# Moving the first loads of a two-layer hybrid block between two DMA-issuing engines

## The chip, the cores and the metric

The kernel runs on one core of a Trainium2 chip. A core has TensorE (PE in the profile, with its weight loads shown apart as PEld), VectorE (DVE), ScalarE (ACT), GpSimd (POOL) and the Sync engine (SP). Transfers are issued by SP or by ScalarE and carried by 16 DMA engines. The metric is the device time of one execution in microseconds. An execution under the profiler gives a trace as well; its times in the text are counted from the start of the profiled span.

## The reference

Two layers work on 512 tokens of width 1024, all in float32. Each layer normalises its input, projects it, mixes tokens (layer A by a chunked spatial gate, layer B by attention with forgetting), attends to 256 memory rows, projects back, and runs a gated feed-forward network. Only the very first step matters here:

```python
h = x
a = rmsnorm(h, ln_mix_pre[0])
mem_n = rmsnorm(mem, ln_mem[0])
proj = a @ w_in_a[0]
u, v, q_mem = proj[..., :768], proj[..., 768:1536], proj[..., 1536:]
...
h = h + rmsnorm(mixed @ w_out[0], ln_mix_post[0])
```

`rmsnorm` scales each token by the inverse root of its mean square and each feature by a gain.

## The kernel before

Activations lie transposed: the features are on the 128 partitions, in eight tiles (`k` = 0 to 7) of 128 features by 512 tokens. `h` holds all eight; it begins as the input `x`. In float32 the products are made from parts. Every operand is split into a high part, rounded to `fp32r`, and the low remainder, and each product is three matmuls: high by high, high by low, low by high. ScalarE writes the high part and VectorE then computes the low one, by `split` for weights (lines 238 and 239: `whi`, `wlo` from `raw`) and by `scaled_parts` for activations (lines 243 and 244: `ahi`, `alo` from `h`, with a gain from the tile `gains` as the scale). The token's own factor of the norm is applied after the products, so these do not wait for the sums of squares.

The work begins with a warm-up: line 82 queues 20 matmuls on a tile of zeros, 256 columns wide (`idle`), on TensorE. ScalarE issues the load of `gains` (all the norms' gains, 48 KB) and then loads its function table ahead of a first tiny activation (`early`). The rest is in `layer_a`. Its first stage computes the two query tiles of the memory attention: two outputs, eight tiles of features each, three products for each pair, so 48 products of 512 columns. Some of the first half are issued as two halves of 256 columns (`HALVES`). The loop goes over halves of the features (`k` 0 to 3, then 4 to 7), inside it over the two outputs, then over `k`, then over the three products; inputs are used in that order.

`query_weights(m, c0, c1)` loads columns of the weights of output `m` and splits them; 128 columns belong to one `k`. `tokens(k0, k1)` loads tiles of `x` and makes their parts. Both queue their loads on SP, in the order of the program. Thus SP's order is: weights 0 for `k` 0 to 3, `x` tiles 0, 1, 2, 3, weights 1 for `k` 0 to 3, weights 0 for `k` 4 to 7, `x` 4 and 5, `x` 6 and 7, weights 1 for `k` 4 to 7, and then the value weights (line 152) and the memory rows (line 345). A tile of `x` is 256 KB, as is one of these pieces of weights.

Behind the first stage come the value products of `value_block` (the tile `v`), and among them the column sums of the squares of `h` (line 288, tile `st`), which need the running sum `acc` that VectorE builds at line 277. `issue_after` and the helper `behind` only set the order in which an engine's instructions are queued; they add no wait for the earlier instruction's end. The framework orders what is left free by a priority that follows the program.

Of the kernel before, what the change touches and what calls it, by code (L numbers as in the profile page):

```python
# [7 lines left out]
F32 = mybir.dt.float32  # L8
F32R = mybir.dt.float32r
BF16 = mybir.dt.bfloat16  # L10
AF = mybir.ActivationFunctionType
# [4 lines left out]
P = 128  # L16
T = 512
D = 1024
KT = 8
# [21 lines left out]
def hybrid(ctx: ExitStack, tc: tile.TileContext, i: dict, out: bass.AP):  # L41
    nc = tc.nc
    cp = ctx.enter_context(tc.tile_pool(name="const", bufs=1))
# [9 lines left out]
    last_load, last_exp, last_parts = [None], [None], [None, None]  # L53

    def name(s):
        n_of[s] = n_of.get(s, 0) + 1
        return f"{s}_{n_of[s]}"

    def act(s, dt=F32R, shape=(P, T)):
        return ap.tile(list(shape), dt, tag="a", name=name(s))  # L60
# [13 lines left out]
    def ps(tag, shape=(P, T), s="ps"):  # L74
        return pp.tile(list(shape), F32, tag=tag, name=name(s), bufs=2 if tag == "tr" else 3)

    V, A, PE, G = nc.vector, nc.scalar, nc.tensor, nc.gpsimd

    def zeros():
        t = plain("zeros", dt=BF16)  # L80
        V.memset(t, 0.0)
        return t

    def idle(n, t, behind=None, width=T):

        def run():
            o = ps("tr", s="idle")
            for _ in range(n):
                PE.matmul(o[:, :width], t[:, :P], t[:, :width], start=True, stop=True)
        if behind is None:  # L90
            return run()
        with tc.issue_after(behind.ins):
            run()

    zero = zeros()
    idle(20, zero, width=T // 2)


    gains = cp.tile([P, 11 * 8 + 8], F32, name="gains")
    nc.scalar.dma_start(gains, i["gains"])  # L100

    def gain(block, k):
        c = block * KT + k
# [17 lines left out]
    avg = cp.tile([P, 1], F32, name="avg")  # L121
# [3 lines left out]
    rms_eps = cp.tile([P, 1], F32, name="rms_eps")  # L125
    V.memset(rms_eps, RMS_EPS)
    early = cp.tile([P, 1], F32, name="early")
    A.activation(early, avg, AF.Copy, scale=2.0)


    def pair_of_parts(n=512, aside=False):
        if aside:
            return act("whi"), act("wlo")
        return (wp.tile([P, max(n, 512)], F32R, tag="hi", name=name("whi"), bufs=8)[:, :n],
                wp.tile([P, max(n, 512)], F32R, tag="lo", name=name("wlo"), bufs=8)[:, :n])

    def cut(pair, w):

        return [(pair[0][:, d : d + w], pair[1][:, d : d + w]) for d in range(0, pair[0].shape[1], w)]
# [98 lines left out]
    def split(src, hi, lo, eng=None):  # L238
        last_parts[:] = A.copy(hi, src), (eng or V).tensor_sub(lo, src, hi)  # L239
# [6 lines left out]
    @contextmanager  # L246
    def behind(some):

        with ExitStack() as s:
            for ins in some:  # L250
                s.enter_context(tc.issue_after(ins.ins))
            yield
# [71 lines left out]
            return [self.sq[0, cols][:, 0, tb * P - cols[0] : (tb + 1) * P - cols[0]]]  # L324


    h = cp.tile([P, KT, T], F32, name="h")
    rbc = cp.tile([P, T], F32, name="rbc")

    def normed_parts(block, k, cols, hi, lo):  # L330
        c0, c1 = cols
        scaled_parts(h[:, k, c0:c1], gain(block, k), hi[:, c0:c1], lo[:, c0:c1])
# [256 lines left out]
    def layer_a():  # L589
# [2 lines left out]
        pre.done = False  # L592
        wq, raws = ([], []), [wp.tile([P, 1024], F32, tag="raw", name=name("raw"), bufs=4) for _ in range(2)]

        def query_weights(m, c0, c1):
            last_load[0] = nc.sync.dma_start(raws[m][:, c0:c1], i["w_a_q"][m][:, c0:c1])
            for c in range(c0, c1, 512):
                pair = pair_of_parts()
                split(raws[m][:, c : c + 512], *pair)
                wq[m].extend(cut(pair, P))  # L600

        def tokens(k0, k1):
            nc.sync.dma_start(h[:, k0:k1, :], i["x"][:, k0:k1, :])
            for k in range(k0, k1):
                normed_parts(G_MIX_PRE, k, FULL, *a[k])

        query_weights(0, 0, 512)
        for k in range(4):
            tokens(k, k + 1)
        query_weights(1, 0, 512)  # L610
        query_weights(0, 512, 1024)
        tokens(4, 6)
        tokens(6, 8)
        last_a = tuple(last_parts)
        query_weights(1, 512, 1024)
# [29 lines left out]
        with tc.tile_pool(name="sgu", bufs=1) as lp:  # L645
# [23 lines left out]
            for half in range(0, KT, 4):  # L669
                for o, w in zip(outs, wq):  # L670
                    for k in range(half, half + 4):
                        for n, (x, y) in enumerate(((0, 0), (0, 1), (1, 0))):
                            first = k == n == 0
                            for c0, c1 in (HALVES if half == 0 and not first else (FULL,)):
                                PE.matmul(o[:, c0:c1], w[k][x], a[k][y][:, c0:c1], start=first,
                                          stop=k == KT - 1 and n == 2, skip_group_check=c1 - c0 < T)
# [110 lines left out]
            for n in range(2):  # L787
# [5 lines left out]
                for g in range(3):  # L793
                    c = bsp[:, 3 * n + g, :]
# [591 lines left out]


    phase = layer_a()

    def memory():  # L1390
# [38 lines left out]
    zero = zeros()  # L1429
# [70 lines left out]
```

## Time and profile before

| | |
|---|---|
| median of 3 runs | 1105.0 us (1104.49 to 1106.13) |
| profiled execution | 1104.96 us |
| its span in the profile | 1103.2 us |
| TensorE busy | 1094.7 us, 99% of the span |
| VectorE, ScalarE busy | 887.8 us, 680.1 us |
| read from HBM | 105.23 MB, 97 GB/s over the span |

A row of the timeline reads: start, time from the first start to the last end of the merged instructions, engine, source line, operation, output and inputs, their number, and in brackets how long the engine had been idle before and what released it. SPq and ACTq are the queues of SP and of ScalarE that issue transfers. A matmul's end is modelled, so its time includes the way through the array: two matmuls that follow each other start closer together than one lasts.

### The profile page before, as it was taken

What the parts mean: (1) busy time and instruction counts of PE and PEld (TensorE: products, weight loads), DVE (VectorE), ACT (ScalarE), POOL (GpSimd) and SP (SyncE); (2) the same over time, 40 slices, a digit from 0 to 9 for tenths busy, and PEclk for the clock granted to TensorE, in tenths of its full rate; (3) what the DMA queues carried; (4) which work ended last, traced back from release to release, by engine and by line L of the source; (5) the groups of instructions that cost most, each with busy time, mean ns of one, the idle gap of its engine ahead of it and who ended that gap; (6) DMA issues with size and microseconds to landing.
All of it is one profiled execution on the core that took longest, in us unless ns stands there. A gap on an engine that the chain in (4) does not pass through costs nothing.

```text
span 1103.2 us, 19498 instructions
## 1 busy us (share of the span) xinstructions
PE 1094.7 (99%) x7363; PEld 1001.1 (91%) x7364; DVE 887.8 (80%) x1750; ACT 680.1 (62%) x1428; POOL 24.4 (2%) x40
## 2 busy tenths in 40 slices
PE   9999999999999999999999999999999999999998
PEld 7998889999899899998988998889999899899996
DVE  7879759997698588797968789868998698588776
ACT  7776578664365254477747788868665266255454
POOL 0000000000000000001000000000000000000000
PEclk9999999999999999999999999999999999999999
DMA  7521331334134133245222654531235134233232
GB/s 269 161 80 54 119 115 39 116 115 136 56 115 144 54 109 115 77 153 175 73 81 61 155 133 121 148 115 40 78 93 157 58 114 132 62 114 116 77 97 77
DMA packets 64021, 118.65 MB, mean 108 GB/s; under 512 B 5236, under 2 KB 40072, under 8 KB 63928
## 3 DMA queue, kind: packets, MB, share of 16 engines
q1 hardware_dynamic: 63032, 116.57, 34.8%
q8 instruction: 58, 0.95, 0.4%
q0 software_dynamic: 192, 0.52, 0.2%
q10 hardware_dynamic: 704, 0.32, 0.1%
q14 instruction: 35, 0.29, 0.1%
HBM read 105.23 MB, written 2.10 MB: 97 GB/s over the span
## 4 chain that ended last, share of the span: by engine, by line
PE 95%; ACT 2%; DVE 2%; DMA 0%; issue 0%; SPq 0%; DVEq 0%; ACTq 0%
PE y L191 10%; PE y L193 10%; PE y L192 10%; PE a L191 5%; PE a L193 5%; PE a L192 5%; PE ps L191 4%; PE ps L193 4%; PE ps L192 4%; PE e L191 3%; PE e L193 3%; PE e L192 3%; PE x L193 3%; PE x L191 3%; PE x L192 3%; PE v L191 2%
## 5 line engine op out<-in xcount | busy, mean ns | idle before, releaser
L239 ACT CAST whi<-raw 128x512 fp32r<-128x512 f32 x460 | 277.9, 621 | 260.7 <-PE y L193 118.5
L239 DVE TENSOR_TENSOR wlo<-raw,whi 128x512 fp32r<-128x512 f32 x460 | 307.4, 690 | 116.6 <-ACT whi L239 114.5
L191 PE MATMUL y<-whi,fhi 128*128 128x512 f32 (+1 forms) x356 | 139.6, 393 | 0.0
L193 PE MATMUL y<-whi,flo 128*128 128x512 f32 (+1 forms) x356 | 139.4, 391 | 0.0
L192 PE MATMUL y<-wlo,fhi 128*128 128x512 f32 (+1 forms) x356 | 139.3, 391 | 0.0
L193 PE MATMUL x<-xshi,wlo 128*128 128x256 f32 x320 | 89.8, 281 | 0.0
L191 PE MATMUL x<-xshi,whi 128*128 128x256 f32 x320 | 89.7, 280 | 0.0
L191 PE MATMUL a<-xshi,whi 128*128 128x256 f32 x320 | 89.7, 281 | 0.0
L192 PE MATMUL a<-xslo,whi 128*128 128x256 f32 x320 | 89.7, 280 | 0.0
L192 PE MATMUL x<-xslo,whi 128*128 128x256 f32 x320 | 89.7, 280 | 0.0
L193 PE MATMUL a<-xshi,wlo 128*128 128x256 f32 x320 | 89.7, 281 | 0.0
L193 PEld LDWEIGHTS y<-whi,flo 128*128 128x128 f32 x356 | 66.9, 188 | 15.6 <-DVE flo L239 0.2
L192 PEld LDWEIGHTS y<-wlo,fhi 128*128 128x128 f32 x356 | 66.9, 188 | 14.8 <-DVE wlo L239 0.2
L191 PEld LDWEIGHTS y<-whi,fhi 128*128 128x128 f32 x356 | 66.9, 188 | 14.7
L191 PE MATMUL ps<-xshi,whi 128*128 128x256 f32 (+1 forms) x224 | 68.4, 305 | 0.0
L192 PE MATMUL ps<-xslo,whi 128*128 128x256 f32 (+1 forms) x224 | 66.6, 298 | 0.0
L193 PE MATMUL ps<-xshi,wlo 128*128 128x256 f32 (+1 forms) x224 | 66.3, 298 | 0.0
L191 PEld LDWEIGHTS a<-xshi,whi 128*128 128x128 f32 x320 | 60.3, 188 | 0.3
L192 PEld LDWEIGHTS a<-xslo,whi 128*128 128x128 f32 x320 | 60.2, 188 | 0.4
L193 PEld LDWEIGHTS x<-xshi,wlo 128*128 128x128 f32 x320 | 60.2, 188 | 0.0
L191 PEld LDWEIGHTS x<-xshi,whi 128*128 128x128 f32 x320 | 60.2, 188 | 0.0
L193 PEld LDWEIGHTS a<-xshi,wlo 128*128 128x128 f32 x320 | 60.2, 188 | 0.0
(303 smaller groups left out, 3080.3 us busy)
## 6 DMA issues: line engine op xcount, KB each, us to landing
raw<-in_w_gate SPq DMA_DIRECT2D x44, 512.0 KB, 3.6
raw<-in_w_up SPq DMA_DIRECT2D x44, 512.0 KB, 3.6
raw<-in_w_down SPq DMA_DIRECT2D x44, 512.0 KB, 4.2
raw<-in_w_out SPq DMA_DIRECT2D x16, 512.0 KB, 3.9
raw<-in_w_b_q SPq DMA_DIRECT2D x8, 512.0 KB, 4.4
raw<-in_w_a_v SPq DMA_DIRECT2D x6, 512.0 KB, 8.2
raw<-in_w_a_u SPq DMA_DIRECT2D x6, 512.0 KB
raw<-in_w_v SPq DMA_DIRECT2D x6, 512.0 KB, 3.5
```

The costliest lines, as they stand in the source:

```text
L191: PE.matmul(o, w[0], x[0], start=start, stop=False, skip_group_check=more)
L192: PE.matmul(o, w[0], x[1], start=False, stop=False, skip_group_check=more)
L193: return PE.matmul(o, w[1], x[0], start=False, stop=stop, skip_group_check=more)
L239: last_parts[:] = A.copy(hi, src), (eng or V).tensor_sub(lo, src, hi)
```

## The change

ScalarE issues `x` tiles 0 and 1 as its first instructions, and tile 3 behind the tiny activation that follows its table load. `gains` moves to SP. The first weights are loaded in two halves of 256 columns (128 KB each), each split by itself; the second half's split is queued behind the parts of tile 1, and the weights of output 1 behind the parts of tile 3. SP's order becomes: weights 0 for `k` 0 and 1, `gains`, weights 0 for `k` 2 and 3, `x` 2, weights 1 for `k` 0 to 3, weights 0 for `k` 4 to 7, and from there on as it was. The warm-up has 16 matmuls in place of 20. In the first stage the three products of a pair are made in the order high by high, low weights by high input, high weights by low input, where the last two stood the other way round.

```diff
-    idle(20, zero, width=T // 2)
+    idle(16, zero, width=T // 2)
...
-    nc.scalar.dma_start(gains, i["gains"])
+    h = cp.tile([P, KT, T], F32, name="h")
+    for k in range(2):
+        nc.scalar.dma_start(h[:, k : k + 1, :], i["x"][:, k : k + 1, :])
...
-    A.activation(early, avg, AF.Copy, scale=2.0)
+    with tc.issue_after(A.activation(early, avg, AF.Copy, scale=2.0).ins):
+        nc.scalar.dma_start(h[:, 3:4, :], i["x"][:, 3:4, :])
...
-        def query_weights(m, c0, c1):
+        def query_weights(m, c0, c1, after=()):
             last_load[0] = nc.sync.dma_start(raws[m][:, c0:c1], i["w_a_q"][m][:, c0:c1])
             for c in range(c0, c1, 512):
-                pair = pair_of_parts()
-                split(raws[m][:, c : c + 512], *pair)
+                n = min(512, c1 - c)
+                pair = pair_of_parts(n)
+                with behind(after):
+                    split(raws[m][:, c : c + n], *pair)
                 wq[m].extend(cut(pair, P))
 
         def tokens(k0, k1):
-            nc.sync.dma_start(h[:, k0:k1, :], i["x"][:, k0:k1, :])
+            if k0 not in (0, 1, 3):
+                nc.sync.dma_start(h[:, k0:k1, :], i["x"][:, k0:k1, :])
             for k in range(k0, k1):
                 normed_parts(G_MIX_PRE, k, FULL, *a[k])
 
-        query_weights(0, 0, 512)
-        for k in range(4):
+        query_weights(0, 0, 256)
+        nc.sync.dma_start(gains, i["gains"])
+        for k in range(2):
             tokens(k, k + 1)
-        query_weights(1, 0, 512)
+        query_weights(0, 256, 512, tuple(last_parts))
+        for k in range(2, 4):
+            tokens(k, k + 1)
+        query_weights(1, 0, 512, tuple(last_parts))
         query_weights(0, 512, 1024)
         tokens(4, 6)
         tokens(6, 8)
...
-                        for n, (x, y) in enumerate(((0, 0), (0, 1), (1, 0))):
+                        for n, (x, y) in enumerate(((0, 0), (1, 0), (0, 1))):
```

More of the change, by code (lines that the diff above doesn't have):

```diff
@@ L324, in sums @@
             return [self.sq[0, cols][:, 0, tb * P - cols[0] : (tb + 1) * P - cols[0]]]
-    h = cp.tile([P, KT, T], F32, name="h")
     rbc = cp.tile([P, T], F32, name="rbc")
```

## The prediction, made before the changed kernel was run

> **What bounds the kernel now.** First the busy times of the page, then the waits of TensorE in the first 10 us, then TensorE's busy time in three stretches.
>
> ```profile
> span 1103.2 us, 19498 instructions
> ...
> PE 1094.7 (99%) x7363; PEld 1001.1 (91%) x7364; DVE 887.8 (80%) x1750; ACT 680.1 (62%) x1428; POOL 24.4 (2%) x40
> ```
> ```profile
> PE ps L675 <- ACT ahi L243: 0.9, 2, 0.5
> PE ps L675 <- DVE alo L244: 0.6, 2, 0.3
> ```
> ```profile
> 5.21:9.13 3.92, 2.46 (x13) 1.74 (x14) 1.00 1.01 362
> 9.13:18.87 9.74, 9.74 (x57) 8.43 (x57) 1.00 1.03 402
> ```
> ```profile
> 9.13:1093.00 1083.87, 1082.76 (x7293) 992.50 (x7294) 878.36 (x1727) 671.53 (x1410) 23.11 (x33) 1.00 0.35 106
> ```
>
> The reader is to see that TensorE is idle for 1.11 us in the whole stretch from 9.13 to 1093 us. All that an edit of the loads can win lies ahead of 9.13, where TensorE waits four times, twice for a high part and twice for a low one. These rows of the timeline show what those waits hang on:
>
> ```profile
> 1.25 3.96 PE L89 MATMUL idle<-zeros 128*128 128x256 bf16 x20 [1.25 <-DVE zeros L81]
> ...
> 4.08 0.62 ACT L239 CAST whi<-raw 128x512 fp32r<-128x512 f32 x1 [1.34 <-DMA raw<-in_w_a_q]
> ...
> 4.73 0.69 DVE L239 TENSOR_TENSOR wlo<-raw,whi 128x512 fp32r<-128x512 f32 x1 [2.43 <-ACT whi L239]
> 4.81 1.34 ACT L243 ACTIVATE ahi<-h,gains 128x512 fp32r<-128x512 f32 x2
> ...
> 5.57 1.42 DVE L244 SCALAR_TENSOR_TENSOR alo<-h,gains,ahi 128x512 fp32r<-128x512 f32 x2
> ...
> 5.58 0.50 PE L675 MATMUL ps<-ahi,whi 128*128 128x512 f32 x1 [0.38 <-ACT ahi L243]
> ...
> 6.37 0.50 PE L675 MATMUL ps<-alo,whi 128*128 128x256 f32 x2 [0.29 <-DVE alo L244]
> ...
> 7.57 1.40 ACT L243 ACTIVATE ahi<-h,gains 128x512 fp32r<-128x512 f32 x2 [1.42 <-DMA h<-in_x]
> ...
> 8.32 1.43 DVE L244 SCALAR_TENSOR_TENSOR alo<-h,gains,ahi 128x512 fp32r<-128x512 f32 x2 [1.34 <-ACT ahi L243]
> 8.34 0.30 PEld L675 LDWEIGHTS ps<-ahi,whi 128*128 128x128 f32 x2 [0.72 <-ACT ahi L243]
> ...
> 10.42 0.39 PE L675 MATMUL ps<-ahi,whi 128*128 128x512 f32 x1
> ...
> 10.85 1.34 ACT L243 ACTIVATE ahi<-h,gains 128x512 fp32r<-128x512 f32 x2 [0.65 <-DMA h<-in_x]
> ...
> 11.61 2.94 DVE L244 SCALAR_TENSOR_TENSOR alo<-h,gains,ahi 128x512 fp32r<-128x512 f32 x4 [0.32 <-ACT ahi L243]
> ...
> 12.38 1.34 ACT L243 ACTIVATE ahi<-h,gains 128x512 fp32r<-128x512 f32 x2 [0.19 <-DMA h<-in_x]
> ...
> 13.29 0.39 PE L675 MATMUL ps<-ahi,whi 128*128 128x512 f32 x1
> ```
>
> The first product starts at 5.58, 0.77 us behind the start of the first `ahi` at 4.81. Seven of the 48 products have started by 9.13; the 57 matmuls from there to 18.87 are the other 41 products (16 in two halves, 25 whole), one each 0.237 us. Without waits the first seven would take 1.66 us, not 3.55: **1.89 us** are lost behind the first product. The largest piece is the third `x` tile: ScalarE stands idle 1.42 us for it and goes on at 7.57.
>
> **The change part by part.** The issue of loads, from the timeline, the chain of waits, SP's waits and the stretches with the bytes moved:
>
> ```profile
> 0.80 0.41 ACTq L100 DMA_DIRECT2D gains<-in_gains  x1
> 0.80 0.40 SPq L596 DMA_DIRECT2D raw<-in_w_a_q  x1
> ...
> 1.25 1.28 ACT L128 ACT_TABLE_LOAD   x1 [1.25 <-PEq L1491]
> ...
> 1.26 1.83 SPq L603 DMA_DIRECT2D h<-in_x  x4
> ...
> 2.54 0.20 ACT L128 ACTIVATE early<-avg 128x1 f32<-128x1 f32 x1
> ...
> 4.29 0.80 SPq L603 DMA_DIRECT2D h<-in_x  x2
> ```
> ```profile
> 2.19 5.36 DMA h<-in_x
> ```
> ```profile
> SPq L603 <- DMA gains<-in_gains: 0.2, 1, 0.2
> ```
> ```profile
> 0.00:5.00 5.00, 3.75 (x20) 2.71 (x20) 1.54 (x7) 2.30 (x4) 1.32 (x7) 1.00 0.57 177
> 5.00:10.00 5.00, 3.53 (x22) 2.60 (x21) 3.52 (x6) 3.54 (x6) 0.00 (x0) 1.00 1.00 367
> 10.00:15.00 5.00, 5.00 (x36) 4.65 (x36) 4.57 (x8) 4.16 (x8) 0.00 (x0) 1.00 1.01 389
> ```
> ```profile
> 47.70 0.41 ACT L239 CAST memv<-memv 128x256 fp32r<-128x256 f32 x1
> 48.13 0.43 DVE L239 TENSOR_TENSOR memv<-memv,memv 128x256 fp32r<-128x256 f32 x1 [0.47 <-ACT memv L239]
> ```
>
> *ScalarE's queue.* Two issues (2 x 0.46 us, the distance of SP's) stand ahead of the table load where one stood, so load and `early` move by 0.46 us, `early` to about 3.0 to 3.2; the issue of tile 3 follows until about 3.65. ScalarE's next instruction, `whi`, waited for its data to 4.08, so this costs nothing; it would if the weights came before 3.65.
>
> *The first tile's parts, T0.* Tile 0 is issued at 0.80, not 1.26: 0.46 us. What must have landed for the first product is 128 + 48 + 256 KB, not 256 + 48 + 256; the 128 KB less are 0.33 us at 389 GB/s. Both gains in full would put the first `ahi` at 4.81 - 0.46 - 0.33 = 4.0. Against that, `gains` is now issued at 1.26 behind the half weights, beside `x` 1, and the first `ahi` needs it. Before, issued at 0.80, it had landed at 4.29 (SP's wait for it ends there); 0.46 later is 4.75. So T0 lies between 4.0 and 4.8; I take **4.6**, near the row of `gains`. First product 5.37, 0.2 earlier.
>
> *The order of products.* Low weights by high input stands second, and needs nothing that is late: while VectorE makes the first `alo` (0.75 us behind the first product), TensorE has two products to do, not one. From T0 = 4.6: high-high 5.37, low-high 5.61, high-low 6.15; then `k` = 1 at 6.39, 6.62 and 6.86, until 7.10. Count and operands are unchanged. Its price is one place: for output 1, `wlo` is needed at its second product.
>
> *The halved weights.* Two splits of 256 columns for one of 512: ScalarE 2 x 0.41 - 0.62 = 0.20 us more, VectorE 2 x 0.43 - 0.69 = 0.17. The second half stands on ScalarE between tiles 1 and 2, at 5.95 to 6.35, inside what was the 1.42 us wait; without that wait it costs 0.2 to 0.4.
>
> *Tile 2.* It keeps its place: issued at 2.19, with 128 + 48 + 128 KB ahead of it on SP and 512 KB on ScalarE's queue, the same 816 KB that stood ahead of it before. Tile 3 now comes beside it rather than behind it. Earliest it is wanted at 6.35, latest I allow 7.57 as now. The two gains in issue time speak for a little earlier, tile 3 beside it against; I take **7.1**. What follows, for both ends: at 6.35 the products of `k` = 2 start at 7.1, those of `k` = 3 at 8.15, output 1 at 8.85 with 0.2 of wait for its `wlo`, the second half at 11.9. There tiles 4 to 7 decide (`ahi` from 10.85 and 12.38, low parts 11.61 to 14.55), since all 2.3 MB ahead of tile 6 are the same bytes at the same 367 to 389 GB/s: the low parts hold the products of output 0 until 14.8, output 1 takes 12 x 0.233 (24 in 13.29 to 18.87), end **17.65, 1.2 us earlier**. At 7.57: `k` = 2 at 8.34, `k` = 3 at 9.35, output 1 at 10.1 instead of 10.42, its `wlo` at 10.4, second half at 13.05 instead of 13.29: **0.25 us earlier**. At 7.1 the same steps lie 0.47 earlier, tiles 4 to 7 take none of it: **0.7 us**.
>
> *The warm-up.* It ended at 5.21; 16 end about 4.7, ahead of any first product. Its four fewer matmuls save nothing at T0 = 4.6, and would have delayed a product before 5.2.
>
> *Behind 18.87.* The nearest thing that could refuse the shift is the sum of squares:
>
> ```profile
> 18.94 4.89 DVE L277 TENSOR_TENSOR acc<-acc,sq 128x512 f32<-128x512 f32 x7
> ```
> ```profile
> 23.77 0.79 PE st L288 x8
> ```
>
> Two of the seven additions for `h` stand before these; five of these seven finish it, at 18.94 + 5 x 0.70 = 22.4. TensorE comes at 23.77, so 1.3 us of shift pass. The sum: 1104.96 - 0.7 = 1104.3. The profiled run is at the median (1105.0), so this stands for both.
>
> **A page beside the rows.** In the rows above the 16 engines are full from 5 us on (share 1.00 to 1.03). The Trainium skill, "DMA: Bandwidth & Descriptors", section "Issuing engines are not separate DMA queues", says that a second issuing engine saves only the sequencer's issue time, since all transfers interleave on the same 16 DMA engines. By it the result would be the first rival below.
>
> **The rivals.**
> 1. *Tile 2 still sets the pace.* All bytes ahead of it are the same, and the engines are full; then the 1.42 us wait stays and only the product order gains: 0.25 us, 1104.7. For it: 2.19 to 7.57 is mostly queueing. Against: the engines move 177 GB/s on average in the first 5 us, so there are holes that a second queue can fill. A quarter.
> 2. *All holes close.* T0 = 4.0, first product 4.8, all 48 products at 0.237: end 16.2, 2.6 us less, 1102.3. It needs tiles 4 to 7 about 1.5 us earlier, which full engines don't give. A tenth at most.
> 3. *SP waits for a completed transfer.* The ninth transfer before, `x` 4 and 5, was held until `gains` had landed (4.29, with 0.2 of wait). If one may have eight in flight, the eleventh now, `x` 6 and 7, waits for one of the first, tile 3 among them (in use at 8.25 before), instead of going at 4.69. Products of tile 6 have 1.5 us of room in the old schedule and 0.8 in the new; 1 us of room exceeded by 0.7 undoes the gain: 1105.0. 0.08.
> 4. *The clock is not up: slower.* The 20 warm-ups run at half rate first:
>
> ```profile
> 1.25 0.82 PE L89 MATMUL idle<-zeros 128*128 128x256 bf16 x3 [1.25 <-DVE zeros L81]
> ```
> ```profile
> 4.61 0.60 PE L89 MATMUL idle<-zeros 128*128 128x256 bf16 x4
> ```
> ```profile
> 4.83 0.38 PE L89 MATMUL idle<-zeros 128*128 128x256 bf16 x2
> ```
>
>    Two more matmuls at the end cost 0.60 - 0.38 = 0.22 for two, 0.11 each, and the last one's own time is 0.38 - 0.11 = 0.27. All 20 take 3.96: with four at the fast distance, (3.96 - 0.27 - 3 x 0.11) / 16 = 0.21 each for the others, about twice as long; the three at the start, in 0.82, agree. The step falls at about 4.5, with the sixteenth. If 16 don't do, a product costs 0.42 and not 0.237. From a first product at 5.4 and half rate until t, the end is 0.44t + 14.5: as before at t = 10.0, 2.2 us late at t = 15.0, and with the whole stage at half rate 5.4 + 48 x 0.42 + 0.1 = 25.7, 6.8 us late, 1111.8. Up to 10.0 the late tiles hide it. Against: 3.3 us of work sufficed, and products fill most of 5.4 to 10.0. 0.07, 0.04 of it over 0.2%.
>
>    The Trainium skill, "TensorE: Matmul & The Clock Gate", Part 1, has the clock rise after a window of about 3.4 us of activity that runs freely; the 3.3 us here agree, and with such a window 16 warm-ups of 3.4 us can just miss it in some executions.
>
> **How the numbers follow.** Forecast, a gain of 0.5 to 1.2 us: 0.5, with a range of its own from 1103.8 to 1104.5. Rival 1: 0.25; rival 2: 0.10; rival 3: 0.08; rival 4: 0.07. The three runs spread over 1.6 us (1104.49 to 1106.13), which I add as 0.8 to either side of the bounds 1103.8 and 1105.0: 1103.0 to 1105.8. Widened to 1102.6 to reach part of rival 2 and to 1106.0 for the milder cases of rival 4, this holds about 8 in 10. About 0.2%, 2.2 us, is what a measurement of this kernel can tell from no change; only rival 2 passes it on the one side (0.08) and the long end of rival 4 on the other (0.05 with an unforeseen new wait behind 18.87). The rest, 0.87, is within.
>
> **What would show it.** Right: first `ahi` near 4.6 and the first product near 5.4; the second group of products low-high without a wait; ScalarE's wait for tile 2 ending near 7.1; the last product of line 675 near 18.1 rather than 18.65, and everything behind it earlier by the same. Wrong: tile 2 at 7.5 or later (rival 1); `ahi` of tiles 4 to 7 well ahead of 10.85 and 12.38 (rival 2); SP idle ahead of `x` 6 and 7 (rival 3); products at 0.42 behind 6 us (rival 4); or a wait of TensorE at line 288 or in the rest of the kernel that was not there.

## The result, and the profile after

| | before | after |
|---|---|---|
| median (lowest to highest) | 1104.88 us (1104.49 to 1106.13, 6 runs) | 1109.38 us (1108.23 to 1110.17, 6 runs) |
| ratio of after to before | | 1.0038 [1.0028, 1.0049] |
| profiled execution | 1104.96 us | 1109.83 us |
| start of the first value product (`v`) in it | 18.87 us | 23.84 us |

The changed kernel is 4.5 us (0.4%) slower. The forecast was 1104.3, so even the sign was wrong. The profiled executions differ by 4.87 us, the starts of the value products by 4.97: all of the loss lies in the first stage, and what lies behind it takes as long as before (1086.0 us for 1086.1). The busy times and TensorE's and ScalarE's waits (engine, line, what it waited for: us in total, times, longest) of after:

```profile
PE 1097.9 (99%) x7360; PEld 1004.1 (91%) x7360; DVE 887.7 (80%) x1751; ACT 679.8 (61%) x1429; POOL 24.4 (2%) x40
```
```profile
PE ps L684 <- ACT ahi L246: 3.4, 2, 2.3
...
ACT ahi L246 <- DMA h<-in_x: 4.1, 2, 3.4
...
ACT whi L242 <- DMA h<-in_x: 1.7, 1, 1.7
```

The reader is to see two things. The four short waits of TensorE have become two, one of them 2.3 us long. And the third row is odd: `whi` is made from weights, yet its wait is put down to a load of `h`, that is, of `x`. ScalarE was not waiting for `whi`'s data: SP too waited for these weights to land, and went on at 4.34. The timeline shows what held ScalarE (start, us, engine, line):

```profile
0.80 0.90 ACTq L102 DMA_DIRECT2D h<-in_x  x2
...
3.03 0.20 ACT L130 ACTIVATE early<-avg 128x1 f32<-128x1 f32 x1
...
4.34 1.07 SPq L608 DMA_DIRECT2D h<-in_x  x2
4.52 0.34 ACTq L131 DMA_DIRECT2D h<-in_x  x1
4.89 0.40 ACT L242 CAST whi<-raw 128x256 fp32r<-128x256 f32 x1 [1.67 <-DMA h<-in_x]
5.21 1.33 ACT L246 ACTIVATE ahi<-h,gains 128x512 fp32r<-128x512 f32 x2
...
5.98 0.79 PE L684 MATMUL ps<-ahi,whi 128*128 128x512 f32 x1 [1.13 <-ACT ahi L246]
...
6.57 0.63 PE L684 MATMUL ps<-ahi,wlo 128*128 128x256 f32 x2
...
7.52 0.72 ACT L246 ACTIVATE ahi<-h,gains 128x512 fp32r<-128x512 f32 x1 [0.69 <-DMA h<-in_x]
...
11.68 0.72 ACT L246 ACTIVATE ahi<-h,gains 128x512 fp32r<-128x512 f32 x1 [3.44 <-DMA h<-in_x]
...
12.45 0.51 PE L684 MATMUL ps<-ahi,whi 128*128 128x256 f32 x2 [2.27 <-ACT ahi L246]
...
23.84 0.28 PE L194 MATMUL v<-whi,ahi 128*128 128x256 f32 x1
```

The tiny activation `early` ends at 3.23. The issue of tile 3 (line 131) is the next thing in ScalarE's queue, and it starts only at 4.52. Until it has been issued, `whi` cannot start. The chain of waits, cut at 13 us (start, us, what), says what released it:

```profile
0.80 3.70 DMA h<-in_x
4.50 0.02 issue
4.52 7.14 DMA h<-in_x
11.66 0.02 issue
11.68 0.72 ACT ahi L246
```

Tile 0 lands at 4.50, and 0.02 us later tile 3 is issued. The compiled instructions of ScalarE name the link (number, line, operation, semaphores it waits for):

```
4 L131 DMA h_98<-in_x 128x512 [waits DMAHW0_49]
6 L246 ACTIVATE ahi_1_126<-h_98,gains_97 128x512 [waits DMAHW2_49]
```

The framework gives the transfers eight completion semaphores in turn (0 to 7), whichever engine issues them, in the order in which it schedules them. In after these are tile 0, weights, `gains`, tile 1, weights, tile 2 and two more pieces of weights, eight in all; tile 3 is the ninth. It takes semaphore 0, that of tile 0, and so waits until tile 0 has landed. The tenth transfer, tiles 4 and 5, and the eleventh, tiles 6 and 7, stand on SP and wait in the same way, for the first weights and for `gains` (SP's waits):

```profile
SPq L608 <- DMA raw<-in_w_a_q: 0.8, 1, 0.8
...
SPq L608 <- DMA gains<-in_gains: 0.4, 1, 0.4
```

Once issued, tile 3 takes 7.14 us to land, at 11.66, and TensorE stands for it until 12.45.

The windows (us, busy time of PE, PEld, DVE, ACT and POOL with the number of instructions, granted clock, DMA share, GB/s) give the sum; first before, then after:

```profile
5.58:18.87 13.29, 12.19 (x70) 10.35 (x71) 11.35 (x18) 10.99 (x20) 0.00 (x0) 1.00 1.03 392
```
```profile
5.98:9.98 4.00, 4.00 (x17) 3.81 (x17) 2.48 (x4) 1.57 (x3) 0.00 (x0) 1.00 1.02 385
9.98:12.45 2.47, 0.20 (x1) 0.00 (x0) 0.02 (x1) 0.77 (x2) 0.00 (x0) 1.00 1.04 417
12.45:23.84 11.39, 11.21 (x54) 9.55 (x55) 10.97 (x18) 11.07 (x21) 0.00 (x0) 0.85 0.89 311
...
13.95:17.35 3.40, 3.26 (x15) 3.15 (x15) 3.40 (x7) 3.40 (x7) 0.00 (x0) 0.50 1.01 363
```

The 48 products took 13.29 us before: 48 x 0.237 = 11.38, and 1.9 of waits. After, they take 17.86. Nine products (17 matmuls: eight products in halves, one whole) take 4.00 us, 1.87 over 9 x 0.237. Then TensorE stops for 2.47 us. The other 39 take 11.39, 2.15 over 39 x 0.237, and most of that is one stretch of 3.4 us, 13.95 to 17.35, at a granted clock of 0.50: half of it, 1.7 us, is lost. So against before: 1.87 + 2.47 + 2.15 - 1.9 = 4.6 us longer, and a start 0.40 later (5.98 for 5.58): 5.0 of the 4.97 seen.

### The profile page after: what moved, and what is told of

Same layout as the page of the kernel before. It is cut to its first block, busy times and chain, and to the rows that moved or that the text cites. A ratio compares the mean times of both kernels' runs of the same rounds, so it can differ in the third digit from the quotient of the medians.

```text
span 1108.1 us, 19494 instructions
## 1 busy us (share of the span) xinstructions
PE 1097.9 (99%) x7360; PEld 1004.1 (91%) x7360; DVE 887.7 (80%) x1751; ACT 679.8 (61%) x1429; POOL 24.4 (2%) x40
## 4 chain that ended last, share of the span: by engine, by line
PE 96%; ACT 2%; DMA 1%; DVE 1%; issue 0%; DVEq 0%; ACTq 0%
PE y L194 10%; PE y L195 10%; PE y L196 10%; PE a L196 5%; PE a L195 5%; PE a L194 5%; PE ps L194 4%; PE ps L196 4%; PE ps L195 4%; PE e L196 3%; PE x L196 3%; PE e L195 3%; PE e L194 3%; PE x L195 3%; PE x L194 3%; PE v L194 2%
## 5 line engine op out<-in xcount | busy, mean ns | idle before, releaser
L242 ACT CAST whi<-raw 128x512 fp32r<-128x512 f32 (+1 forms) x461 | 277.8, 619 | 261.4 <-PE y L196 118.6
L242 DVE TENSOR_TENSOR wlo<-raw,whi 128x512 fp32r<-128x512 f32 (+1 forms) x461 | 306.8, 686 | 117.1 <-ACT whi L242 114.6
L195 PEld LDWEIGHTS x<-xslo,whi 128*128 128x128 f32 x320 | 60.3, 188 | 0.0
```

The costliest lines, as they stand in the source:

```text
L195: PE.matmul(o, w[0], x[1], start=False, stop=False, skip_group_check=more)
```

## The experiments

Three theories stood at first: that the late tile 3 makes the loss, by its place in the order of issue; that it is the engine whose queue it stands in, or the way ScalarE's own order moves; and that it is the clock, which four warm-up matmuls less no longer bring up. The medians and 95% intervals; "parts" is when ScalarE starts the high part of tile 3 (or of tiles 2 and 3, where they come together), "values" the start of the first value product, and "rest" the profiled execution's time less that start. Before, these three were 7.57, 18.87 and 1086.1.

| run | median, us | ratio to before | parts | values | rest |
|---|---|---|---|---|---|
| after | 1109.38 | 1.0038 [1.0028, 1.0049] | 11.68 | 23.84 | 1086.0 |
| x3_on_sp | 1105.01 | 1.0000 [0.9990, 1.0009] | 6.57 | 18.02 | 1086.8 |
| warm20 | 1109.42 | 1.0041 [1.0026, 1.0055] | 10.91 | 22.16 | 1086.0 |
| x3_early | 1105.32 | 1.0002 [0.9993, 1.0012] | 7.19 | 19.21 | 1086.2 |
| before_x3_act | 1109.02 | 1.0035 [1.0023, 1.0046] | 10.78 | 20.40 | 1086.9 |
| x3_late_sp | 1107.92 | 1.0031 [1.0018, 1.0043] | 10.58 | 22.07 | 1085.9 |
| one_load | 1106.46 | 1.0014 [1.0004, 1.0023] | 8.67 | 20.14 | 1086.3 |
| before_x3_kept | 1106.11 | 1.0015 [1.0006, 1.0024] | 8.37 | 20.20 | 1086.0 |
| before_warm16 | 1105.59 | 1.0008 [0.9999, 1.0016] | 7.93 | 19.58 | 1086.0 |
| sp_late_sums | 1105.82 | 1.0008 [0.9999, 1.0016] | 6.77 | 18.96 | 1086.4 |
| sp_late_sums20 | 1105.57 | 1.0005 [0.9996, 1.0014] | 6.29 | 17.50 | 1088.1 |
| sp20_sums_first | 1104.39 | 0.9995 [0.9987, 1.0004] | 6.79 | 17.89 | 1086.9 |
| gains_first | 1103.92 | 0.9990 [0.9981, 0.9999] | 7.36 | 18.52 | 1085.4 |

### Tile 3 back on SP

The changed kernel, but SP issues tile 3 behind tile 2, and nothing of it stands on ScalarE:

```diff
-    with tc.issue_after(A.activation(early, avg, AF.Copy, scale=2.0).ins):
-        nc.scalar.dma_start(h[:, 3:4, :], i["x"][:, 3:4, :])
+    A.activation(early, avg, AF.Copy, scale=2.0)
...
-            if k0 not in (0, 1, 3):
+            if k0 not in (0, 1):
```

> The changed kernel with the load of tile 3 back on SP, behind tile 2, and nothing else undone. Theory L (tile 3 comes late, because ScalarE issues it at 4.52 and it then stands behind all that SP has issued by that time): the ahi of tile 3 starts at 7.5 to 8.6, not 11.68, TensorE's idle 2.27 us ahead of it is gone, the second stretch at half clock (13.9 to 17.4) does not come, and the time is 1104.3 to 1105.8. Theory C (16 warm-ups are too few, and the products at half rate are the loss): the first products stay at about 0.42 us each up to 9 or 10 us and the time stays above 1107.

It is as fast as before, 1105.01: this one load makes the whole loss of 4.4 us. Two rows of its timeline and one of its waits:

```profile
6.57 1.37 ACT L245 ACTIVATE ahi<-h,gains 128x512 fp32r<-128x512 f32 x2 [0.17 <-DMA h<-in_x]
...
18.02 0.28 PE L193 MATMUL v<-whi,ahi 128*128 128x256 f32 x1
```
```profile
PE st L290 <- DVE acc L279: 0.7, 1, 0.7
```

Tiles 2 and 3 are used from 6.57 on, a microsecond earlier than before (7.57) and than expected, and the value products start 0.85 us earlier. Yet the time is the old one. TensorE now waits 0.73 us at the column sums (line 290; 288 before) for VectorE's `acc`. So the rest of the change brings about the gain that was forecast up to the value products (0.85 us for 0.7), and 0.73 of it is taken back at the sums of squares.

### The old warm-up

The changed kernel with `idle(20` for `idle(16`, 20 warm-up matmuls.

> The changed kernel with 20 warm-ups again, nothing else undone. Theory L: tile 3 is as late as in the changed kernel (ahi at 11 to 12), TensorE does the nine products before it sooner and waits longer, the time stays at 1107 to 1110. Theory C: the products run at 0.237 us from the first one on and the time comes back to 1104 to 1105.5.

Full rate from the first products, and the median does not move: 1109.42. What the early products gain they lose again in front of tile 3, where the stop is longer (two rows of the timeline, one of the waits):

```profile
6.29 0.41 PE L684 MATMUL ps<-ahi,wlo 128*128 128x256 f32 x2
...
10.91 0.72 ACT L246 ACTIVATE ahi<-h,gains 128x512 fp32r<-128x512 f32 x1 [3.48 <-DMA h<-in_x]
```
```profile
PE ps L684 <- ACT ahi L246: 3.6, 2, 2.8
```

The two halves of the second product take 0.41 us, where after's took 0.63 (its row at 6.57). The four warm-ups are not the cause of the loss. (The profiled execution, 1108.14, is the fastest of this kernel's five; its tile 3 came 0.77 earlier than in the profile of after.)

### Tile 3 early on ScalarE

The same load on the same engine, but ahead of the table load, as ScalarE's third issue:

```diff
-    for k in range(2):
+    for k in (0, 1, 3):
         nc.scalar.dma_start(h[:, k : k + 1, :], i["x"][:, k : k + 1, :])
```

(The issue behind `early` is left out.)

> The changed kernel with tile 3 issued by ScalarE as its third instruction, ahead of the table load, at about 1.7 us. Theory L in its reading that the time of issue is what counts, not the issuing engine: tile 3 lands with or ahead of tile 2, its ahi by 8.3, no stop of 2 us, time 1104.3 to 1105.8. A theory that ScalarE's queue is served behind SP's as long as SP has work: ahi of tile 3 stays at 10 us or later, and the time at 1107 or more. Theory C: above 1107 either way.

1105.32, no loss that can be measured. ScalarE's queue itself does not make tile 3 late; the time of the issue does. A row shows what is late next:

```profile
5.17 1.34 ACT L245 ACTIVATE ahi<-h,gains 128x512 fp32r<-128x512 f32 x2 [0.45 <-DMA gains<-in_gains]
```

With the block on ScalarE gone, the first `ahi` waits for `gains` until 5.17. After had hidden this: there ScalarE was held until 4.89 in any case.

### The kernel before, with tile 3 alone on ScalarE

The kernel before, where the load behind `early` is issued by ScalarE and left out on SP; first with nothing else, then with the split of the weights of output 1 held behind the parts of tile 3, as in after:

```diff
-            nc.sync.dma_start(h[:, k0:k1, :], i["x"][:, k0:k1, :])
+            if k0 != 3:
+                nc.sync.dma_start(h[:, k0:k1, :], i["x"][:, k0:k1, :])
...
-                split(raws[m][:, c : c + 512], *pair)
+                with behind(after):
+                    split(raws[m][:, c : c + 512], *pair)
...
-        query_weights(1, 0, 512)
+        query_weights(1, 0, 512, tuple(last_parts))
```

(The second and third piece belong to before_x3_kept alone.)

> The kernel before with one part of the change alone: tile 3 is issued by ScalarE behind the activation that follows its table load (at 2.8 us or later). Theory L: slower by as much as the issue is late; if it has to wait for an earlier transfer to land, issued at about 4.3 and in use at about 11, 2 to 4 us slower (1107 to 1109); if it goes at 2.8, it lands about where it did and the time is within 0.7 us of before. Theory C: 20 warm-ups, so no change, within 0.7 us of before.

> The kernel before with tile 3 issued by ScalarE behind its table load, as in before_x3_act, but with the split of weights 1 queued behind the parts of tile 3, as in both the kernel before and the changed one; in before_x3_act the framework had put it ahead of the parts of tile 2. Theory time: issued at 2.3 it lands about where it did, ahi of tile 2 and 3 by 8.5 to 9, and the time is 1104.8 to 1106; the 4 us of before_x3_act came from ScalarE's order (it waited for weights 1, landed at 9.1, with tile 2 behind). Theory queue: it stays above 1107.

The first one is 4.2 us slower than before (its profiled execution, 1107.33, is its fastest), and taken alone would have seemed to prove that ScalarE's queue is bad. But ScalarE issued tile 3 at 2.34 here, without a wait, since the first weights are one load, and fewer transfers come before it. The loss is another:

```profile
2.34 0.35 ACTq L130 DMA_DIRECT2D h<-in_x  x1
...
9.12 0.62 ACT L241 CAST whi<-raw 128x512 fp32r<-128x512 f32 x1 [2.07 <-DMA raw<-in_w_a_q]
9.64 0.72 ACT L245 ACTIVATE ahi<-h,gains 128x512 fp32r<-128x512 f32 x1
```

With the load moved, the framework queued the split of the weights of output 1 ahead of the high part of tile 2, and ScalarE stood 2.07 us for weights that nobody needed yet. With ScalarE's order kept, the time is 1106.11: 2.9 us of the 4.2 were this. What is left, 1.3 us, missed the expectation narrowly. There tiles 2 and 3, issued at about 2.2 and 2.34, are used from 8.37, not from 7.57: side by side they came later than one behind the other. Its clock is a second possible reason: from 7.73 to 11.14 the granted clock of this profile is 0.50, and how much of the 1.3 us each makes stays open.

### Late, but on SP

The changed kernel with no load of tile 3 on ScalarE. SP issues it behind two pieces of weights and tiles 4 and 5:

```diff
...
+            if k0 == 3:
+                nc.sync.dma_start(raws[1][:, 0:512], i["w_a_q"][1][:, 0:512])
+                nc.sync.dma_start(raws[0][:, 512:1024], i["w_a_q"][0][:, 512:1024])
+                nc.sync.dma_start(h[:, 4:6, :], i["x"][:, 4:6, :])
+                nc.sync.dma_start(h[:, 3:4, :], i["x"][:, 3:4, :])
...
```

> The changed kernel, but tile 3 issued by SP, right behind x 4 and 5 and ahead of x 6 and 7, so at about the time (4.5 to 5) at which ScalarE issued it, and from the other engine. Theory time (what counts is how much has been issued when the load of tile 3 is issued, not who issues it): ahi of tile 3 at 10.3 to 11.7, TensorE stops for 1.5 to 2.5 us ahead of it, time 1107 to 1110, as in the changed kernel. Theory queue (ScalarE's queue gets less than its share while SP's is full): tile 3 lands by 9, time under 1107.

```profile
4.81 0.43 SPq L613 DMA_DIRECT2D h<-in_x  x1
...
10.58 0.72 ACT L245 ACTIVATE ahi<-h,gains 128x512 fp32r<-128x512 f32 x1 [2.47 <-DMA h<-in_x]
...
22.07 0.28 PE L193 MATMUL v<-whi,ahi 128*128 128x256 f32 x1
```

Issued by SP at 4.81, tile 3 is used at 10.58, and the time is 1107.92: two thirds of the loss with nothing late on ScalarE. Four profiles taken together show how the stage hangs on tile 3: the value products start 11.3 to 12.2 us behind the start of tile 3's parts (11.68 to 23.84 in after, 10.91 to 22.16 in warm20, 10.58 to 22.07 here, 8.67 to 20.14 in the next). In before_x3_act, where ScalarE had already split the weights of output 1, it was 9.6 (10.78 to 20.40).

### Eight transfers instead of nine

The changed kernel with the first weights in one load, so that tile 3 is the eighth transfer and takes a semaphore that is free:

```diff
-        query_weights(0, 0, 256)
+        query_weights(0, 0, 512)
...
-        query_weights(0, 256, 512, tuple(last_parts))
```

> The changed kernel with one edit: the first weights come as one load of 512 columns and one split again, so one transfer less stands ahead of tile 3, which then waits for no earlier transfer's landing. ScalarE still issues it behind the activation that follows its table load. Theory time: issued at 3.2 and not at 4.52, beside or behind tile 2 and weights 1, ahi of tile 3 between 7 and 8.7, no stop of 2 us, time 1104.5 to 1106. Theory queue: tile 3 stays at 9.5 or later in spite of the earlier issue, time 1107 or more.

```profile
2.34 0.34 ACTq L131 DMA_DIRECT2D h<-in_x  x1
4.98 0.62 ACT L242 CAST whi<-raw 128x512 fp32r<-128x512 f32 x1 [1.76 <-DMA raw<-in_w_a_q]
...
8.67 0.72 ACT L246 ACTIVATE ahi<-h,gains 128x512 fp32r<-128x512 f32 x1 [0.99 <-DMA h<-in_x]
```

In the queue of ScalarE nothing has changed place but the second split, which is gone, and tile 3 is issued at 2.34, not 4.52. That is ahead of `early`, which starts at 3.02: the issue does not wait for the activation in front of it to be done. The time falls by 2.9 of the 4.5 us, although the undivided weights now hold the first product back, to 6.51, and the granted clock is 0.50 from 7.33 to 10.74. Together with x3_early and x3_late_sp this shows the wait of the ninth transfer as the main cause. The time stays 0.5 us over what was expected; how much of that each of the two costs makes is not shown.

### Where the gain of the rest goes

x3_on_sp had left 0.85 us of gain that the column sums took back. Four kernels asked whether it can be kept. In sp_late_sums the column sums come one piece of the value products later, in sp_late_sums20 with 20 warm-ups besides; before_warm16 is the kernel before with 16 warm-ups; sp20_sums_first is x3_on_sp with 20 warm-ups and, on VectorE, the memory rows' additions queued behind the last addition for `h`.

```diff
-        pieces(2)
+        pieces(3)
         pre.finish(FULL)
...
-        pieces(2)
+        pieces(1)
```
```diff
-            self.last = V.tensor_add(self.acc, self.acc, sq)
+            with behind(after):
+                self.last = V.tensor_add(self.acc, self.acc, sq)
...
-    norm = mem_sums(memt)
+    norm = mem_sums(memt, (pre.last,))
```

> The changed kernel with tile 3 on SP (as x3_on_sp) and the column sums of the squares put one piece of value products (12 matmuls, 1.4 us) later. Theory: in x3_on_sp the value products started 0.85 us earlier than before (18.02 to 18.87), and TensorE gave 0.73 of it back waiting for the sum of squares at 23.16; with the later place that wait is gone and the time is 0.5 to 0.9 us below x3_on_sp: 1104.1 to 1104.5. Rival: another wait takes it up further on (the norm's factor for the value tiles, whose three PSUM buffers are then held longer), and the time stays at 1104.8 to 1105.2.

> sp_late_sums with 20 warm-ups in place of 16. In the profiled execution of sp_late_sums all products up to 10.2 us ran at 0.42 us. Theory clock (the 0.8 us by which it was above x3_on_sp came from 16 warm-ups that did not bring the clock up before the products): products at 0.237 us from about 5.5 on, value products from about 18.0, time 1104.0 to 1104.7. Theory sums (the later place of the sums costs it further on): the time stays at 1105.3 to 1106 with the clock up.

> The kernel before with 16 warm-ups in place of 20, nothing else. If four warm-ups fewer often leave the clock at half for the first products: 0.5 to 1.7 us slower (1105.3 to 1106.5), with products at 0.42 us in the trace. If 16 are as good as 20: 1104.5 to 1105.1, as before. In the changed kernel neither would show, since tile 3 holds TensorE until 12.4 us.

> x3_on_sp with 20 warm-ups and VectorE's additions for the memory rows queued behind the last addition for h (in x3_on_sp one of them stood ahead of it, 0.7 us). Theory: the wait of 0.73 us at the column sums goes, and with the clock up the 0.85 us won at the start come through: 1104.0 to 1104.5. Rival: the gain is taken up by the next wait again, 1104.7 to 1105.1.

sp_late_sums missed: 1105.82, no gain. Its profile ran at half rate until 10.2 us, which left two explanations, and sp_late_sums20 tells them apart. The clock is up there, the value products start at 17.50, 1.4 us earlier than before, and the time is still 1105.57, because a new wait has come:

```profile
PE rb L259 <- POOL r L262: 1.6, 1, 1.6
```

With the sums later, the norm's factor `r` from GpSimd is later, and TensorE waits 1.6 us for it. Moved back by one piece, the sums cost that. Moving VectorE's own order instead takes both waits away: sp20_sums_first reaches 1104.39, within what was expected. It isn't separable from before by its interval, and since it also has 20 warm-ups, its 0.6 us under x3_on_sp are not the order's alone. In its profile the value products start 0.98 us earlier than before and the execution ends only 0.21 earlier, so most of the gain is taken back here too. One wait of TensorE, far behind the first stage, is new:

```profile
PE e L193 <- ACT s L1082: 0.5, 1, 0.5
```

before_warm16 was at half rate in its profile until 10.4 us, and the value products started 0.7 us later than before; its median is 0.6 us higher, with an interval that still touches no change. So 16 warm-ups cost nothing or up to 0.16% there.

### The fastest version

sp20_sums_first with `gains` first on ScalarE again, then tile 0, and tile 1 on SP:

```diff
-    for k in range(2):
+    nc.scalar.dma_start(gains, i["gains"])
+    for k in range(1):
...
-            if k0 not in (0, 1):
+            if k0:
...
-        nc.sync.dma_start(gains, i["gains"])
```

> sp20_sums_first with gains as ScalarE's first load and tile 0 its second; tile 1 goes back to SP behind the first half of the weights. In the changed kernel gains landed at about 5.1, and the first ahi waited for it or for ScalarE; here gains has landed by 4.2, the first ahi starts at 4.3 to 4.6, the first product at 5.1 to 5.4, and the time is 0 to 0.4 us below sp20_sums_first. If the engines' throughput alone sets the start, it is the same as sp20_sums_first within 0.2.

```profile
5.83 1.34 ACT L246 ACTIVATE ahi<-h,gains 128x512 fp32r<-128x512 f32 x2 [2.02 <-DMA h<-in_x]
...
18.52 0.28 PE L194 MATMUL v<-whi,ahi 128*128 128x256 f32 x1
```

1103.92 us (1103.60 to 1104.62, 11 runs), 1.0 us or 0.1% under before: the only version whose interval lies wholly below before, and only just (0.9981 to 0.9999); among twelve kernels tried, one such interval can come by chance. It was expected at 0 to 0.4 us below sp20_sums_first and came 0.5 below, but not for the reason expected. The wait for `gains` is gone, but tile 0 now lands late, the first `ahi` comes at 5.83 (4.81 before) and the value products start later than in sp20_sums_first, 18.52 for 17.89. They start 0.35 us earlier than before, and the rest of the kernel is 0.7 shorter (1085.4 for 1086.1). The windows behind 30 us, first of gains_first, then of sp20_sums_first:

```profile
30.00:1092.00 1062.00, 1060.93 (x7137) 971.95 (x7137) 858.23 (x1694) 652.16 (x1374) 21.44 (x32) 1.00 0.34 103
```
```profile
30.00:1092.00 1062.00, 1060.54 (x7129) 971.01 (x7129) 856.90 (x1693) 651.52 (x1373) 21.63 (x32) 1.00 0.34 103
```

TensorE is idle 1.07 us there (1062.00 - 1060.93) against 1.46, and the wait of 0.5 us at line 193, which sp20_sums_first has and gains_first has not, accounts for the difference. But from the value products to the end gains_first is 1.5 us shorter than sp20_sums_first (1085.4 for 1086.9), and where the rest of that comes from stays open.

## Why the prediction was wrong

- **The step that failed: "the issue of tile 3 follows until about 3.65".** It came at 4.52. The prediction knew the mechanism, in its third rival: eight transfers in flight, the ninth held. But it put the wait on `x` 6 and 7, the eleventh, at 0.7 us with a chance of 0.08, and didn't ask which transfer was the ninth. At its own distance of 0.46 us from issue to issue that was tile 3: eight others, two on ScalarE and six on SP, go by about 3.1, and tile 3 was to follow at 3.65. Halving the first weights had made the eighth a ninth. What stands behind the blocked issue on ScalarE (`whi`, and so everything) wasn't asked either. one_load, with one transfer fewer, is 2.9 of the 4.5 us faster.
- **The second: "Tile 3 now comes beside it rather than behind it".** The working gave tile 2 a landing time, from both ends, and tile 3 none. It landed at 11.66, behind the 512 KB of tiles 4 and 5, which SP had issued at 4.34 and which landed at 10.23. A tile that is issued later than others of its kind needs its own line in the sum; x3_on_sp, with tile 3 in the old place, is 4.4 us faster than after.
- **T0, a term of the wrong size.** 4.6 was forecast, 5.21 came, held by the same issue until 4.86. Where nothing blocked ScalarE and the first loads were those of after, it lay between 4.74 (sp_late_sums20) and 5.18 (sp20_sums_first), in the late ones because of `gains` (5.17 in x3_early): forecast to have landed at 4.75, `gains` held SP until 5.08 in after.
- **Tile 2 was forecast at 7.1** and used at 7.52 in after, just the mark of the first rival (7.5 or later). But that holds for this one profile: with the same first loads it is used at 6.71 in warm20, at 6.57 in x3_on_sp and at 6.29 in sp_late_sums20. The working took 2.19 to 7.57 before as queueing behind bytes. The traces record sixteen completions for each load, and the last one counts: for tile 2 fifteen were in by 6.78 before and the last at 7.54; in after 6.27 and 7.50, in x3_on_sp 6.29 and 6.54. So 0.76 us of the wait that the forecast began from was one late completion in one execution, and why it was late is open. The term had no effect, since tile 3 came later still.
- **The order of products was right.** Low weights by high input stands second and doesn't wait (5.98, 6.57, 6.99 for the first three).
- **The clock** (fourth rival, 0.07) was seen: nine products at 0.42 to 0.44 us. It was not the cause: warm20 takes it away, and the median stays. The second half-rate stretch, 13.95 to 17.35, stands behind the stop, as it does in warm20 (11.18 to 14.59, behind a stop of 2.79) and in x3_late_sp (11.52 to 14.94, behind 1.91). Its 1.7 us are part of the loss, and that the stop brings it about is argued from these three.
- **"1.3 us of shift pass" at the column sums was wrong.** On VectorE an addition for the memory rows stands ahead of the last one for `h`, which is thus the sixth of the seven and not the fifth: in before it starts at 22.53 and ends at about 23.2, some 0.3 us before TensorE begins to load `acc` for the sums at 23.5, and not 1.3. x3_on_sp pays 0.73 for a shift of 0.85. Even without the late tile, the forecast gain of 0.7 would have been about 0.1.

## What to carry to other kernels

When a load moves to another queue, count it among all transfers of the program, not those of its queue: the framework's completion semaphores are few and shared, and an issue that has to wait for one blocks the whole compute engine that issues it. Give each moved load a landing time of its own, from its time of issue and the bytes issued before it, and look up which instruction wants it. And where a stage gets faster, follow the other engine's queue up to the next meeting point, in its order: here VectorE's order of additions took back 0.73 of 0.85 us until it was changed too.

## What the hardware showed besides

**A load issued late moves late, though its queue is free.** Packets, MB and share of the 16 engines by queue in after, 4.9 to 7.5 us and then 7.5 to 9.5; q1 is SP's queue, q10 is ScalarE's with tile 3 alone:

```profile
q1 hardware_dynamic: 443, 0.85, 97.4%
q10 hardware_dynamic: 1, 0.00, 0.0%
...
q1 hardware_dynamic: 168, 0.58, 72.2%
q10 hardware_dynamic: 125, 0.23, 31.1%
```

From 4.9 to 7.5 tile 3, issued at 4.52, moves one packet, while SP's queue moves 443; then it moves 125 within 2 us, and its last 19 from 9.5 to 11.5. The Trainium skill, "DMA: Bandwidth & Descriptors", section "Queues, rings and completion order", says that each engine takes turns between its queues packet by packet. By it tile 3 would, as an estimate, have had about half of the rate from the start; this trace disagrees for the first 2.6 us. Here the loads landed in the order of their issue, whichever the queue: the last weights (issued at 3.14) at 8.85, tiles 4 and 5 (4.34) at 10.23, tile 3 (4.52) at 11.66, tiles 6 and 7 (5.08) at 11.94. In before_x3_kept, with tiles 2 and 3 issued within 0.2 us on the two queues, the later tile 2 (8.37 for 7.57) fits with sharing. What decides between the two isn't settled here.

**The clock falls after a stop of 2.3 us.** In after TensorE stopped for 2.27 us (12.45), and 1.5 us after it went on the granted clock fell to 0.50 for 3.4 us, as the windows showed. The trace's record of the clock has one stretch from 10.53 to 13.95 at 1.00, and then the one at 0.50; TensorE stood still for 1.92 us of the first, from 10.53 to 12.45. The Trainium skill, "TensorE: Matmul & The Clock Gate", Part 1, has a window of about 3.4 us, with which the trace agrees, and puts half rate behind an idle window, where here a window with 1.92 us of idle time was enough. The column of the granted clock says 1.00 from 5.98 to 9.98 all the same, where nine products took 4.00 us: the record begins only at 10.53, and ahead of it one goes by the distance of the matmuls.
